# Two-layer diffusion backbone on one core: weight splits and modulation accumulation in instructions of 1024 columns in place of 512

## The chip, the core and the metric

The program runs on one core of one Trainium2 chip. The metric is the time of one execution on the device in microseconds (us), as the median of several runs. The work is fp32 throughout, and every input comes from device memory in each execution.

## The reference

Two layers work on 256 latent tokens (and in layer 0 on 256 context tokens beside them), with a model width of 1024 and a hidden width of 2816. A layer is a half-step SwiGLU FFN, a token mixer (layer 0: neighbourhood attention; layer 1: a short gated convolution), and a second half-step FFN. Each sub-layer is modulated by rows that come from a conditioning vector.

```python
m = (silu(c) @ ada_w[i] + ada_b[i]).reshape(B, N_MOD, 1, D)      # nine rows a layer
...
def half_step_ffn(x, shift, scale, gate, w_in, w_out, g, b):
    a, u = split(modulate(x, shift, scale) @ w_in, 2)             # x * (1 + scale) + shift
    y = (silu(a) * u) @ w_out
    return layer_norm(ALPHA * x + 0.5 * gate * y, g, b)
...
x = half_step_ffn(x, m[0], m[1], m[2], ffn_w_in[i, 0], ffn_w_out[i, 0], ...)
x = post_norm_update(x, mixer(modulate(x, m[3], m[4])), m[5], 1.0, ...)
x = half_step_ffn(x, m[6], m[7], m[8], ffn_w_in[i, 1], ffn_w_out[i, 1], ...)
```

In attention a latent token reads a window of the latent grid and all context keys in one softmax. The weights are read once each: 5632 columns in and 2816 rows out for each of four FFNs, 3072 and 1024 columns for each mixer, and 9216 columns of `ada_w` a layer.

## The kernel before

**Split products.** TensorE (PE) multiplies in a reduced fp32 form (`fp32r`). To keep the accuracy, each operand is stored as a high part, rounded to that form, and a low part, the rest. A product is three matmuls: high by high, high by low and low by high (`mmu`, lines 152 to 159). A weight comes in units of 256 rows by 512 columns, which lie in a tile as 128 partitions by 1024 columns (`wunit`). The program calls the raw unit `w1r`, `w2r`, `wor` and so on, its high part `w1h`, its low part `w1l`. ScalarE (ACT) makes the high part (line 178) and VectorE (DVE) the low part (line 181), each in two instructions of 512 columns, as `W_HI` and `W_LO` are 2. There are four buffers for raw units and five for each part (`WB`), with a few more in some phases.

**Activations.** Between sub-layers a normalised tile is transposed on PE into PSUM (`hT`), scaled and shifted by ACT in four instructions of 128 columns (`h`, line 340), and split by ACT (`hTh`, line 105) and DVE (`hTl`, line 106). `panels` then runs over panels of 512 columns of the FFN's first weight (256 for silu, 256 for the factor), four units each, for two token tiles; `lead_in` gives the order of the first two panels. `done` of `gated` makes `sil`, the product of both halves (DVE, line 386), which PE transposes (line 394). `out_gemm` multiplies by the second weight, `w2`, or by `wo` after a mixer.

**The first FFN** holds its activations transposed (`f0_mm`) and starts while its own modulation is computed (`start_step`). The units of its first two panels are split in that phase.

**Modulation rows.** The other rows are made in the background by `ada`: 128 rows of `ada_w` for one modulation vector (1024 columns) are loaded as `ar`, and DVE multiplies them by one element of silu(c) per partition and adds them up in `acc`, a first product (line 241) and seven updates (line 243) for each vector, each in two halves of 512 columns. Ones on PE then sum `acc` over the partitions. A step of it is released after so many matmul groups (`tick`, the background rate).

**Attention** (layer 0) runs in steps of a head and a query tile: scores S on PE (line 814), a bias and the row's maximum on DVE, the exponential on ACT (line 818) and its scaling `pr` (line 820), four transposes PT on PE (line 832), the split into `pT` (lines 105 and 106), and the values o (PE, lines 844 and 845), collected by ACT as `osum` (line 850). The key, query and value projections of later heads (`wkv`, `wq`; `kT` is the transposed key, line 769) and the first units of `wo` are filled in between these steps.

**The order of the work.** PE's instructions stand in the order of the program text, by hand. Those of the other engines are ordered by a scheduler from priorities; `tc.high_priority` moves a block of them forward by a number of places. Weight splits are moved by `w_early`, the activation's splits by `LN_EARLY`, the softmax and what follows it by `S_EARLY`, `P_EARLY` and `V_EARLY`. Each engine runs its own queue from front to back.

Of the kernel before, what the change touches and what calls it, by code (L numbers as in the profile page):

```python
# [9 lines left out]
F32 = mybir.dt.float32  # L10
F32R = mybir.dt.float32r
AF = mybir.ActivationFunctionType
ALU = mybir.AluOpType
# [3 lines left out]
P = 128  # L17
D = 1024
# [34 lines left out]
AHEAD = 3  # L53
P_EARLY = 70
V_EARLY = 70
W_HI = 2
W_LO = 2
NA = (1, 2, 1, 0, 0, 0)
NB = (2, 2, 1, 0, 0, 0)
E0 = (0,)  # L60
# [4 lines left out]
def backbone_kernel(  # L65
# [6 lines left out]
    nc = tc.nc  # L72
# [8 lines left out]
    hp = phase.__enter__()  # L81
# [2 lines left out]
    w_early = [0]  # L84
    ext = [1, 0]
    ada_late = [0]

    def nm(s):
        uid[0] += 1
        return f"{s}_{uid[0]}"  # L90
# [54 lines left out]
    def set_background(gen, rate):  # L145
        background[:] = [gen, rate, 0.0]
# [15 lines left out]
    def wunit(srcs, kn, s):  # L162

        raw = wp.tile([P, UN], F32, tag="wr", bufs=WB[0], name=nm(s + "r"))
        ext[1] += 1
        if ext[0] and ext[1] % (5 + ext[0]) in (E0 if ext[0] == 1 else E2):
            hi = hp.tile([P, UN], F32R, tag="whx", bufs=ext[0], name=nm(s + "h"))
            lo = hp.tile([P, UN], F32R, tag="wlx", bufs=ext[0], name=nm(s + "l"))
        else:
            hi = wp.tile([P, UN], F32R, tag="wh", bufs=WB[1], name=nm(s + "h"))  # L170
            lo = wp.tile([P, UN], F32R, tag="wl", bufs=WB[2], name=nm(s + "l"))
        rv, hv, lv = (t[:, :kn * 512].rearrange("p (a b) -> p a b", a=kn) for t in (raw, hi, lo))
        with tc.high_priority(offset=w_early[0]):
            for src, c in srcs:
                sync.dma_start(rv[:, :, c:c + src.shape[2]], src)
            m = kn * 512
            for a in range(0, m, m // W_HI):
                nc.scalar.activation(hi[:, a:a + m // W_HI], raw[:, a:a + m // W_HI], AF.Copy)  # L178
            for a in range(0, m, m // W_LO):
                b = a + m // W_LO  # L180
                nc.vector.tensor_tensor(out=lo[:, a:b], in0=raw[:, a:b], in1=hi[:, a:b].bitcast(F32), op=ALU.subtract)  # L181
        return hv, lv

    def wrows(w, r0, n, c0, s):
        src = w[r0:r0 + n * P, c0:c0 + 512].rearrange("(k p) n -> p k n", p=P)
        return wunit([(src, 0)], n, s)

    def wpair(w, u, c0, c1, s):
        if c1 == c0 + 256:
            return wrows(w, u * UK * P, UK, c0, s)  # L190
        src = w[u * UK * P:(u + 1) * UK * P, :].rearrange("(k p) n -> p k n", p=P)
        return wunit([(src[:, :, c0:c0 + 256], 0), (src[:, :, c1:c1 + 256], 256)], UK, s)
# [7 lines left out]
    cst = cp.tile([P, KC, 32], F32, tag="cst", name="cst")  # L200
# [10 lines left out]
    ones = cp.tile([P, 32], F32, tag="ones", name="ones")  # L211
# [4 lines left out]
                            in1=idv[:, 1, :, 0:2], op=ALU.add)  # L216
# [7 lines left out]
    def ada(vecs):  # L224


        acc = {}
        for l, m in dict.fromkeys((l, m) for l, m, _ in vecs):
            for k in range(KC):
                w = hp.tile([P, D], F32, tag="ar", bufs=3, name=nm("ar"))  # L230
                sync.dma_start(w, ada_w[l, k * P:(k + 1) * P, m * D:(m + 1) * D])
                for i, vec in enumerate(vecs):
                    if vec[:2] != (l, m):
                        continue
                    if k == 0:
                        acc[i] = [hp.tile([P, 512], F32, tag="acc", bufs=4, name=nm("acc")) for _ in range(2)]
                    sc = cst[:, k, vec[2]:vec[2] + 1]
                    for h in range(2):
                        src, a = w[:, h * 512:(h + 1) * 512], acc[i][h]
                        if k == 0:  # L240
                            nc.vector.tensor_scalar(a, src, sc, None, op0=ALU.mult)
                        else:
                            nc.vector.scalar_tensor_tensor(out=a, in0=src, scalar=sc, in1=a,  # L243
                                                           op0=ALU.mult, op1=ALU.add)
                yield 1
        n = 2 * len(vecs)
        bt = hp.tile([P, 512], F32, tag="adab", name=nm("adab"))
        for i, (l, m, v) in enumerate(vecs):
            sync.dma_start(bt[64 * i:64 * i + 64],
                           bass.AP(ada_b.tensor, ada_b.offset + (l * 9 + m) * D, [[512, 2], [0, 32], [1, 512]]))  # L250
        yield 1
        yield 1
        yield 1
        rows = hp.tile([P, 512], F32, tag="adar", name=nm("adar"))
        ps = tpb("ada")
        for i in range(len(vecs)):
            for h in range(2):
                j = 2 * i + h
                nc.tensor.matmul(ps[32 * j:32 * j + 32, :], ones, acc[i][h], start=True, stop=True)
        nc.vector.tensor_tensor(out=rows[:32 * n], in0=ps[:32 * n], in1=bt[:32 * n], op=ALU.add)  # L260
        for i, (l, m, v) in enumerate(vecs):
            sync.dma_start(scr[l][v, m * D:(m + 1) * D].rearrange("(a b) -> a b", b=512),
                           rows[64 * i:64 * i + 64:32, :])
        yield 1

    def stream(*groups):
        for g in groups:
            yield from ada(g)
# [91 lines left out]
    def panels(cols, w, hTs, order, done, s):  # L360

        units, banks = {}, {}
        for t, p, u in order:
            if (p, u) not in units:
                units[p, u] = wpair(w, u, *cols[p], s)
            if (t, p) not in banks:
                banks[t, p] = mmb(s, t)
            hi, lo = units[p, u]
            mmu(banks[t, p], [(*hsl(hTs[t], UK * u + i), hi[:, i], lo[:, i]) for i in range(UK)], u == 0, u == KU - 1)
            if u == KU - 1:  # L370
                done(p, t, banks.pop((t, p)))
            yield
            tick()
# [71 lines left out]


    w_in, w_out = ffn_w_in[0, 0], ffn_w_out[0, 0]
    ab0 = [hp.tile([P, 512], F32, tag="acc", bufs=4, name=nm("ab0")) for _ in range(2)]
    for h in range(2):
        nc.vector.memset(ab0[h], 0.0)  # L450
    xt = []
    for t in range(4):
        if t < 2:
# [103 lines left out]
    for q, (k0, n) in enumerate(steps):  # L557
        nxt = start_step(*steps[q + 1]) if q < 4 else iter(())
        for g in range(6):
# [9 lines left out]
    sync.dma_start(win_sb, win_mask)  # L569
    sync.dma_start(rope, rope_tab.rearrange("(t p) a b -> p t a b", p=P))  # L570
    w_early[0] = W_EARLY
    set_background(stream([(0, 2, 0), (0, 2, 1)], [(0, 3, 0), (0, 3, 1)], [(0, 4, 0), (0, 4, 1)],
                          [(0, 5, 0), (0, 6, 0)], [(0, 7, 0), (0, 8, 0)], [(1, 0, 0)]), 0.45)
    ada_late[0] = 0
# [287 lines left out]
    hp = phase.__enter__()  # L862
# [35 lines left out]
    for i in range(len(steps) + LAG + V_LAG):  # L898
# [13 lines left out]
        n = int(credit)  # L912
# [10 lines left out]
        j = i - LAG - V_LAG  # L923
# [8 lines left out]
    hp = phase.__enter__()  # L932
# [20 lines left out]
    w = sc_w_in[0]  # L953
# [104 lines left out]
```

## Time and profile before

| before | |
|---|---|
| three runs, median | 1293.48 us (1292.49 to 1294.41) |
| the profiled execution's own time | 1290.21 us |
| its span on the core | 1288.4 us |
| mean granted clock of TensorE | 0.996 |
| loaded from device memory | 267.93 MB |
| DMA packets' time on the main queue, share of 16 engines' span | 66.9% |

The profile is of one execution, and its durations are in microseconds unless they say ns. Busy time is counted per engine: PE (matmul), PEld (PE's weight load, which overlaps the matmuls), DVE, ACT, POOL (GpSimd). A group of instructions names the line, the engine, the operation, the tiles (written <- read, without their numbers), the shape and the count; behind the bar stand its busy time, the mean of one in ns, and the idle time of the engine in front of them with what ended most of it. In a list of waits a row is engine, tile and line <- what released it, then the total, the number of waits and the longest. In a timeline a row has the start, the length, the engine, the line, the operation and tiles, and a count of instructions that follow each other; in brackets is the wait before it. Instructions of DVE and ACT overlap in their records, so a start-to-start distance is shorter than a length.

### The profile page before, as it was taken

How to read it: one execution, taken by the hardware profiler on the slowest of the kernel's cores; microseconds unless marked ns; L12 is line 12 of the kernel's file. 1: busy time of each engine (PE TensorE's matmuls, PEld its weight loads, DVE VectorE, ACT ScalarE, POOL GpSimd, SP SyncE). 2: the span in 40 equal slices, each digit the busy share in tenths (PEclk: the TensorE clock that was granted, in tenths of full speed). 3: DMA queues.
4: the chain of work that ended last, by engine and by line, in shares of the span. 5: the costliest groups of instructions: out<-in, count | busy, mean ns of one | idle time of the engine just before them, and what ended most of it. 6: DMA issues, size and time to landing. Idle time of an engine off the chain costs nothing.

```text
span 1288.4 us, 17192 instructions
## 1 busy us (share of the span) xinstructions
PE 1256.5 (98%) x5890; PEld 1005.4 (78%) x5890; DVE 954.7 (74%) x1683; ACT 591.0 (46%) x1148; POOL 40.4 (3%) x69
## 2 busy tenths in 40 slices
PE   7999999999999999988999999999999999999997
PEld 4787778788778877766787787887788877788886
DVE  3599877595658767788997888867878688855545
ACT  2433132412326456677554535645435645655431
POOL 0000000000001111120000000000000000000000
PEclk9999999999999999989999999999999999999999
DMA  9978668484622744464998988677887764676641
GB/s 285 284 238 260 187 187 289 153 299 150 216 66 85 217 90 90 92 149 130 314 333 267 325 315 298 205 220 222 290 298 244 211 218 147 214 213 187 226 158 50
DMA packets 204018, 271.26 MB, mean 211 GB/s; under 512 B 30028, under 2 KB 149300, under 8 KB 203930
## 3 DMA queue, kind: packets, MB, share of 16 engines
q1 hardware_dynamic: 203930, 270.16, 66.9%
q8 instruction: 46, 0.75, 0.2%
q14 instruction: 42, 0.34, 0.1%
HBM read 267.93 MB, written 2.17 MB: 210 GB/s over the span
## 4 chain that ended last, share of the span: by engine, by line
PE 81%; DVE 7%; DMA 6%; ACT 3%; issue 1%; SPq 1%; POOL 0%; DVEq 0%; ACTq 0%
PE w L156 15%; PE w L157 14%; PE w L159 14%; PE f L537 6%; PE f L539 6%; PE f L538 6%; DMA w1r<-in_ffn_w_in_dram 4%; DVE w1l L181 2%; PE wkv L156 2%; PE wkv L159 2%; PE wkv L157 2%; PE wc L156 2%; PE wc L157 2%; PE wc L159 2%; DMA ar<-in_ada_w_dram 1%
## 5 line engine op out<-in xcount | busy, mean ns | idle before, releaser
L178 ACT ACTIVATE w1h<-w1r 128x512 fp32r<-128x512 f32 x352 | 203.1, 626 | 185.7 <-PE w L159 71.4
L181 DVE TENSOR_TENSOR w1l<-w1r,w1h 128x512 fp32r<-128x512 f32 x352 | 227.6, 685 | 66.7 <-ACT w1h L178 63.5
L156 PE MATMUL w<-w1h,hTh 128*128 128x512 f32 x528 | 210.8, 399 | 3.3 <-ACT hTh L105 3.3
L243 DVE SCALAR_TENSOR_TENSOR acc<-ar,cst,acc 128x512 f32<-128x512 f32 x266 | 187.5, 746 | 33.6 <-DMA ar<-in_ada_w_dram 33.3
L157 PE MATMUL w<-w1l,hTh 128*128 128x512 f32 x528 | 207.0, 392 | 0.0
L156 PE MATMUL w<-w2h,gh 128*128 128x512 f32 (+1 forms) x446 | 175.4, 394 | 0.0
L157 PE MATMUL w<-w2l,gh 128*128 128x512 f32 (+1 forms) x446 | 173.4, 389 | 0.0
L178 ACT ACTIVATE w2h<-w2r 128x512 fp32r<-128x512 f32 x176 | 101.5, 624 | 140.9 <-PE w L159 122.2
L159 PE MATMUL w<-w1h,hTl 128*128 128x512 f32 x528 | 163.4, 391 | 0.7 <-DVE hTl L106 0.7
L181 DVE TENSOR_TENSOR w2l<-w2r,w2h 128x512 fp32r<-128x512 f32 x176 | 114.0, 686 | 42.1 <-ACT w2h L178 41.4
L537 PE MATMUL f<-h0h,w1h 128*128 128x512 f32 x352 | 139.3, 396 | 0.0
L539 PE MATMUL f<-h0l,w1h 128*128 128x512 f32 x352 | 137.8, 392 | 0.0
L538 PE MATMUL f<-h0h,w1l 128*128 128x512 f32 x352 | 137.8, 391 | 0.0
L159 PE MATMUL w<-w2h,gl 128*128 128x512 f32 (+1 forms) x446 | 136.3, 387 | 0.0
L156 PEld LDWEIGHTS w<-w1h,hTh 128*128 128x128 f32 x528 | 99.2, 188 | 27.2 <-ACT hTh L105 4.6
L159 PEld LDWEIGHTS w<-w1h,hTl 128*128 128x128 f32 x528 | 98.9, 188 | 23.9 <-DVE hTl L106 1.5
L157 PEld LDWEIGHTS w<-w1l,hTh 128*128 128x128 f32 x528 | 99.2, 188 | 20.3 <-DVE w1l L181 0.3
L156 PEld LDWEIGHTS w<-w2h,gh 128*128 128x128 f32 x446 | 83.7, 188 | 21.8 <-issue 1.7
L159 PEld LDWEIGHTS w<-w2h,gl 128*128 128x128 f32 x446 | 83.3, 188 | 18.8
L157 PEld LDWEIGHTS w<-w2l,gh 128*128 128x128 f32 x446 | 83.7, 188 | 17.4
L537 PEld LDWEIGHTS f<-h0h,w1h 128*128 128x128 f32 x352 | 66.2, 188 | 17.9 <-issue 4.1
L539 PEld LDWEIGHTS f<-h0l,w1h 128*128 128x128 f32 x352 | 66.2, 188 | 14.4
(176 smaller groups left out, 1703.1 us busy)
## 6 DMA issues: line engine op xcount, KB each, us to landing
w1r<-in_ffn_w_in_dram SPq DMA_DIRECT2D x352, 256.0 KB
ar<-in_ada_w_dram SPq DMA_DIRECT2D x128, 512.0 KB
w2r<-in_ffn_w_out_dram SPq DMA_DIRECT2D x88, 512.0 KB
ar<-in_ada_w_dram SPq DMA_DIRECT2D x32, 256.0 KB
wkvr<-in_na_w_qkv_dram SPq DMA_DIRECT2D x32, 256.0 KB
wcr<-in_sc_w_in_dram SPq DMA_DIRECT2D x32, 256.0 KB
wqr<-in_na_w_qkv_dram SPq DMA_DIRECT2D x8, 512.0 KB
bias<-in_na_rpb_dram SPq DMA_DIRECT2D x64, 64.0 KB
```

The source lines that it names most:

```text
L156: nc.tensor.matmul(ps, lh, rh, start=first and i == 0, stop=False)
L157: nc.tensor.matmul(ps, lh, rl, start=False, stop=False)
L159: nc.tensor.matmul(ps, ll, rh, start=False, stop=last and i == n - 1)
L178: nc.scalar.activation(hi[:, a:a + m // W_HI], raw[:, a:a + m // W_HI], AF.Copy)
L181: nc.vector.tensor_tensor(out=lo[:, a:b], in0=raw[:, a:b], in1=hi[:, a:b].bitcast(F32), op=ALU.subtract)
L243: nc.vector.scalar_tensor_tensor(out=a, in0=src, scalar=sc, in1=a, op0=ALU.mult, op1=ALU.add)
L537: nc.tensor.matmul(ps, lh, hT0[k][0], start=(k == 0), stop=False)
L538: nc.tensor.matmul(ps, ll, hT0[k][0], start=False, stop=False)
L539: nc.tensor.matmul(ps, lh, hT0[k][1], start=False, stop=(k == KC - 1))
```

## The change

A unit of a weight is split by one ACT instruction and one DVE instruction of 1024 columns where `whole[0]` is set, and by two of each of 512 columns otherwise. `whole[0]` is off until the first FFN's early panels (its first two) have their units, and it is off for panel 0 of every later `panels` (three FFNs and the convolution's first weight). `acc` becomes one tile of 1024 columns for a vector, with two buffers in place of four halves; a product or an update is one instruction. PE reads the two halves of `acc` as before. The start's `ab0` takes one of these tiles and one memset.

```diff
-W_HI = 2
-W_LO = 2
...
+    whole = [False]
...
             m = kn * 512
-            for a in range(0, m, m // W_HI):
-                nc.scalar.activation(hi[:, a:a + m // W_HI], raw[:, a:a + m // W_HI], AF.Copy)
-            for a in range(0, m, m // W_LO):
-                b = a + m // W_LO
+            n = m if whole[0] else 512
+            for a in range(0, m, n):
+                nc.scalar.activation(hi[:, a:a + n], raw[:, a:a + n], AF.Copy)
+            for a in range(0, m, n):
+                b = a + n
                 nc.vector.tensor_tensor(out=lo[:, a:b], in0=raw[:, a:b], in1=hi[:, a:b].bitcast(F32), op=ALU.subtract)
...
                     if k == 0:
-                        acc[i] = [hp.tile([P, 512], F32, tag="acc", bufs=4, name=nm("acc")) for _ in range(2)]
-                    sc = cst[:, k, vec[2]:vec[2] + 1]
-                    for h in range(2):
-                        src, a = w[:, h * 512:(h + 1) * 512], acc[i][h]
-                        if k == 0:
-                            nc.vector.tensor_scalar(a, src, sc, None, op0=ALU.mult)
-                        else:
-                            nc.vector.scalar_tensor_tensor(out=a, in0=src, scalar=sc, in1=a,
-                                                           op0=ALU.mult, op1=ALU.add)
+                        acc[i] = hp.tile([P, D], F32, tag="acc", bufs=2, name=nm("acc"))
+                    sc, a = cst[:, k, vec[2]:vec[2] + 1], acc[i]
+                    if k == 0:
+                        nc.vector.tensor_scalar(a, w, sc, None, op0=ALU.mult)
+                    else:
+                        nc.vector.scalar_tensor_tensor(out=a, in0=w, scalar=sc, in1=a, op0=ALU.mult, op1=ALU.add)
...
-                nc.tensor.matmul(ps[32 * j:32 * j + 32, :], ones, acc[i][h], start=True, stop=True)
+                nc.tensor.matmul(ps[32 * j:32 * j + 32, :], ones, acc[i][:, h * 512:(h + 1) * 512], start=True, stop=True)
...
             if (p, u) not in units:
+                whole[0] = p > 0
                 units[p, u] = wpair(w, u, *cols[p], s)
+                whole[0] = True
...
     w_early[0] = W_EARLY
+    whole[0] = True
```

The order of PE's instructions does not change. On ACT and DVE some do. In the rows below an instruction is line, operation, tile written <- tiles read, with the tiles' numbers and the size; line numbers of the changed kernel are one to four lower.

The **first place** is ACT's queue in attention, from about 545 to 559 us of the profiled execution. `woh` is the high part of a unit of `wo`, `kr` and `v` belong to the key and value projection of later heads, `S`, `pr` and `mx` to the softmax. Before:

```order
L178 ACTIVATE woh_5253<-wor_5252 128x512 x2
L756 ACTIVATE kr_4971<-wkv_4885 128x256
L105 ACTIVATE v_4973<-wkv_4885 128x4x64
L105 ACTIVATE pT_4892<-PT_4976 128x4x128
L105 ACTIVATE pT_4926<-PT_4983 128x4x128
L818 ACTIVATE pr_4946,mx_4944<-S_4935,mx_4944 128x512
L818 ACTIVATE pr_4953,mx_4951<-S_4936,mx_4951 128x512
L820 ACTIVATE pr_4946<-pr_4946,mx_4944 128x512
L850 ACTIVATE osum_4999<-o_4990 64x256
L820 ACTIVATE pr_4953<-pr_4953,mx_4951 128x512
L178 ACTIVATE woh_5374<-wor_5373 128x512
```

And in the changed kernel:

```order
L178 ACTIVATE woh_4982<-wor_4981 128x1024
L756 ACTIVATE kr_4706<-wkv_4620 128x256
L104 ACTIVATE v_4708<-wkv_4620 128x4x64
L104 ACTIVATE pT_4627<-PT_4711 128x4x128
L104 ACTIVATE pT_4661<-PT_4718 128x4x128
L178 ACTIVATE woh_5101<-wor_5100 128x1024
L850 ACTIVATE osum_4734<-o_4725 64x256
L818 ACTIVATE pr_4681,mx_4679<-S_4670,mx_4679 128x512
L818 ACTIVATE pr_4688,mx_4686<-S_4671,mx_4686 128x512
L820 ACTIVATE pr_4681<-pr_4681,mx_4679 128x512
L820 ACTIVATE pr_4688<-pr_4688,mx_4686 128x512
L104 ACTIVATE pT_4767<-PT_4769 128x4x128
```

The unit `woh`, which followed the softmax, now stands ahead of it as a whole, and so does `osum`, which stood between the two scalings.

The **second place** is ACT's queue at the entry of layer 1's first FFN, at about 800 us, where the first `h` is made. Before:

```order
L178 ACTIVATE w1h_7452<-w1r_7451 128x512 x2
L178 ACTIVATE w1h_7498<-w1r_7497 128x512 x2
L178 ACTIVATE w1h_7514<-w1r_7513 128x512
L340 ACTIVATE h_7353<-hT_7348,gcol_6975 128x128 x4
L340 ACTIVATE h_7367<-hT_7362,gcol_6975 128x128
L105 ACTIVATE hTh_7354<-h_7353 128x512
```

And in the changed kernel:

```order
L178 ACTIVATE w1h_7018<-w1r_7017 128x512 x2
L178 ACTIVATE w1h_7064<-w1r_7063 128x1024
L178 ACTIVATE w1h_7078<-w1r_7077 128x1024
L337 ACTIVATE h_6921<-hT_6916,gcol_6575 128x128 x4
L337 ACTIVATE h_6935<-hT_6930,gcol_6575 128x128
L104 ACTIVATE hTh_6922<-h_6921 128x512
```

Of the unit that stands directly in front of `h`, one half stood there before, and the whole now.

The **third place** is DVE's queue in the first panels of layer 0's second FFN, at about 617 us, in front of the first `hTl` of the second token tile. Before:

```order
L181 TENSOR_TENSOR w1l_5702<-w1r_5700,w1h_5701 128x512 x2
L181 TENSOR_TENSOR w1l_5718<-w1r_5716,w1h_5717 128x512 x2
L386 TENSOR_TENSOR sil_5669<-sil_5669,w_1047_5611 128x256
L241 TENSOR_SCALAR acc_5650<-ar_5648,cst 128x512
L241 TENSOR_SCALAR acc_5651<-ar_5648,cst 128x512
L243 SCALAR_TENSOR_TENSOR acc_5650<-ar_5731,cst,acc_5650 128x512
L106 TENSOR_TENSOR hTl_5679<-h_5677,hTh_5678 128x512
```

And in the changed kernel:

```order
L181 TENSOR_TENSOR w1l_5419<-w1r_5417,w1h_5418 128x1024
L181 TENSOR_TENSOR w1l_5433<-w1r_5431,w1h_5432 128x1024
L385 TENSOR_TENSOR sil_5386<-sil_5386,w_1034_5330 128x256
L239 TENSOR_SCALAR acc_5369<-ar_5367,cst 128x1024
L241 SCALAR_TENSOR_TENSOR acc_5369<-ar_5444,cst,acc_5369 128x1024
L105 TENSOR_TENSOR hTl_5396<-h_5394,hTh_5395 128x512
```

Ahead of `hTl` stand the same operations, with the update of `acc` as a whole where only its first half stood there before.

More of the change, by code (lines that the diff above doesn't have):

```diff
@@ L447, in backbone_kernel @@
     w_in, w_out = ffn_w_in[0, 0], ffn_w_out[0, 0]
-    ab0 = [hp.tile([P, 512], F32, tag="acc", bufs=4, name=nm("ab0")) for _ in range(2)]
-    for h in range(2):
-        nc.vector.memset(ab0[h], 0.0)
+    ab0 = hp.tile([P, D], F32, tag="acc", bufs=2, name="ab0")
+    nc.vector.memset(ab0, 0.0)
+    ab0 = [ab0[:, h * 512:(h + 1) * 512] for h in range(2)]
     xt = []
```

## The prediction

> **What bounds the kernel now.** I read the page's busy times first, then the groups of instructions with shapes kept apart, then what TensorE (PE) waited for, then the clock by stretch, and only then single instructions around PE's waits.
>
> ```profile
> PE 1256.5 (98%) x5890; PEld 1005.4 (78%) x5890; DVE 954.7 (74%) x1683; ACT 591.0 (46%) x1148; POOL 40.4 (3%) x69
> PE 81%; DVE 7%; DMA 6%; ACT 3%; issue 1%; SPq 1%; POOL 0%; DVEq 0%; ACTq 0%
> L181 DVE TENSOR_TENSOR w1l<-w1r,w1h 128x512 fp32r<-128x512 f32 x352 | 227.6, 685 | 66.7 <-ACT w1h L178 63.5 <-DMA w1r<-in_ffn_w_in_dram 0.4
> L157 PE MATMUL w<-w1l,hTh 128*128 128x512 f32 x528 | 207.0, 392 | 0.0
> L157 PE MATMUL w<-w2l,gh 128*128 128x512 f32 x434 | 170.3, 392 | 0.0
> ```
>
> PE is busy for 98% of the span. The matmuls that read a split weight's low part (w1l, w2l) never had PE idle in front of them: 0.0 us in both groups. So the 227.6 us that VectorE (DVE) spends on w1l are hidden behind PE, and making them cheaper gains nothing by itself.
>
> ```profile
> PE ada L490 <- DMA ar<-in_ada_w_dram: 3.8, 4, 1.9
> PE xT L500 <- DMA x<-in_x_dram: 3.7, 2, 2.3
> PE w L156 <- ACT hTh L105: 3.3, 3, 2.0
> PE ctp L209 <- DMA crow<-in_c_ctx_dram: 2.6, 1, 2.6
> PE kT L769 <- DVE pT L106: 2.0, 2, 1.6
> PE o L845 <- DVE pT L106: 1.6, 3, 0.6
> ...
> 540.00:560.00 20.00, 16.72 (x100) 12.77 (x99) 17.07 (x37) 17.87 (x41) 4.44 (x5) 0.96 0.51 88
> 560.00:580.00 20.00, 19.41 (x102) 14.97 (x100) 14.54 (x33) 12.98 (x29) 4.39 (x6) 0.87 0.64 164
> ```
>
> The first rows are what PE waited for (total, times, longest). Three of the four longest are loads at the start or a transposed activation; then come kT and o, inside attention, which wait for DVE's split of the transposed probabilities. The last two rows are stretches (length, busy us and instructions of PE, weight load, DVE, ScalarE (ACT), GpSimd, then granted clock, DMA share, GB/s). The clock is below 1 there. The missing 0.04 and 0.13 of 20 us are 3.4 us of PE time, which at half rate is 6.8 us of throttled clock. What this kernel can still gain lies in such short waits and in this dip, some 15 us in all; nowhere else does an instruction of DVE or ACT set the time.
>
> **The change part by part. Prices first.**
>
> ```profile
> 603.45 2.48 DVE L181 TENSOR_TENSOR w1l<-w1r,w1h 128x512 fp32r<-128x512 f32 x4
> 605.85 0.68 DVE L304 SCALAR_TENSOR_TENSOR res<-wo,gate 128x512 f32<-128x512 f32 x1
> 614.84 0.41 DVE L386 TENSOR_TENSOR sil<-sil,w 128x256 f32<-128x256 f32 x1
> 615.18 0.88 DVE L241 TENSOR_SCALAR acc<-ar,cst 128x512 f32<-128x512 f32 x2
> 615.97 0.75 DVE L243 SCALAR_TENSOR_TENSOR acc<-ar,cst,acc 128x512 f32<-128x512 f32 x1
> 616.63 0.69 DVE L106 TENSOR_TENSOR hTl<-h,hTh 128x512 fp32r<-128x512 f32 x1
> ...
> 616.11 0.68 ACT L178 ACTIVATE w1h<-w1r 128x512 fp32r<-128x512 f32 x1
> 616.63 0.68 ACT L105 ACTIVATE hTh<-h 128x512 fp32r<-128x512 f32 x1
> 557.63 0.41 ACT L105 ACTIVATE oT<-osum 128x256 fp32r<-128x256 f32 x1
> 557.93 0.60 ACT L105 ACTIVATE kTh<-kT 128x512 fp32r<-128x512 f32 x1
> ```
>
> Queued instructions overlap, so a price is start to start. On DVE four splits take 605.85 - 603.45 = 2.40 us, 0.60 each; the 256-column product takes 615.18 - 614.84 = 0.34. That is 1.02 ns a column and 0.08 fixed, so 1024 columns are estimated at 1.12 us against 1.20 for two halves. An acc update takes 616.63 - 615.97 = 0.66; for the whole the bounds are 1.18 (only columns added) and 1.32 (nothing saved), and I take 1.24. The two first products take 0.79 together, the whole between that and 0.71. On ACT a half takes 616.63 - 616.11 = 0.52 and 256 columns 557.93 - 557.63 = 0.30: 0.96 for a whole against 1.04.
>
> The change merges 304 pairs of splits on ACT and on DVE, and 152 pairs of acc on DVE (counted in the programs' order). Saved are 304 x 0.08 = 24 us of ACT and 456 x 0.08 = 36 us of DVE, off the path, since PE's 0.0 us above hide them. The DMAs are as many, of the same sizes. The early panels and each panel 0 keep 512 columns. The merged memset of ab0 stands in a start where PE waits for loads: nothing.
>
> What is on the path is the other side: whatever stands behind a whole has to wait 0.44 us longer on ACT and up to 0.52 (a split) or 0.6 (an acc) on DVE, and a low part can't begin before the whole high part is written.
>
> ```profile
> 799.51 0.63 ACT L178 ACTIVATE w1h<-w1r 128x512 fp32r<-128x512 f32 x1 [2.12 <-DMA w1r<-in_ffn_w_in_dram]
> 800.05 1.84 ACT L340 ACTIVATE h<-hT,gcol 128x128 f32<-128x128 f32 x5
> 802.46 0.50 PE L156 MATMUL w<-w1h,hTh 128*128 128x512 f32 x1 [2.02 <-ACT hTh L105]
> 1085.21 3.75 ACT L178 ACTIVATE w1h<-w1r 128x512 fp32r<-128x512 f32 x7 [4.79 <-DMA w1r<-in_ffn_w_in_dram]
> 1091.31 0.50 PE L156 MATMUL w<-w1h,hTh 128*128 128x512 f32 x1 [0.64 <-ACT hTh L105]
> 617.37 0.74 PE L159 MATMUL w<-w1h,hTl 128*128 128x512 f32 x2 [0.32 <-DVE hTl L106]
> 589.64 0.39 PE L845 MATMUL o<-pT,v 128*128 128x256 f32 x1 [0.42 <-DVE pT L106]
> 706.64 0.44 PE L394 MATMUL gT<-ident,sil 128*128 128x128 f32 x2 [0.56 <-DVE sil L386]
> ```
>
> *At 800 us* ACT waits 2.12 us for a weight's load, splits its first half, and only then does the h that PE needs. Now the whole stands there (the second place shown in the change): +0.44, behind a wait of PE that is already open, so all of it counts. If the load comes earlier, as some ada loads are moved past it, this could be -1.5 (about one load's turn); I keep +0.44, the row that is there. *At 1085* seven halves (3.64) become three wholes and two halves (3.92): +0.28. *At 617* hTl has in front of it two wholes of w1l (-0.16), the first product (nothing) and a whole acc (+0.58): +0.4. *At 589* a whole woh stands ahead of two pT where halves alternated with them: +0.4. *At 706* the second sil stands behind a whole acc (+0.58), three wholes ahead of it gave back 0.24; a first pair at 694 has its split start 0.2 later: +0.5 together. If each of these were hidden again, they would be 0; if each were followed by the DVE step behind it, about twice as much.
>
> *Attention, 550 to 559 us:*
>
> ```profile
> 551.28 0.71 ACT L818 ACTIVATE pr<-S,mx 128x512 f32<-128x512 f32 x1
> 552.74 0.28 PE L845 MATMUL o<-pT,v 128*128 128x256 f32 x1
> 553.85 0.66 PE L832 MATMUL PT<-ident,pr 128*128 128x128 f32 x4
> 555.17 0.28 PE L845 MATMUL o<-pT,v 128*128 128x256 f32 x1
> 558.52 1.11 PE L769 MATMUL kT<-ident,kr 128*128 128x128 f32 x4 [1.56 <-DVE pT L106]
> 559.56 0.79 PE L810 MATMUL S<-kTh,qTh 64*128 64x512 f32 x2
> ```
>
> In the new order ACT's osum, which reads the o that ends at 553.0, stands ahead of the softmax pr, which began at 551.28 (first place shown). So the softmax begins some 1.5 to 2 us later, and PE's transposes PT at 553.85 wait about 1.3. But the two woh halves that stood between it and the kT at 558.52 are gone from there, so the 1.56 us there shrink; followed by hand through ACT and DVE, kT comes at about 559.0: +0.5. The bounds are -1 (kT gains all that was moved away) and +1.5.
>
> The sum of these: 0.44 + 0.28 + 0.4 + 0.4 + 0.5 + 0.5 = +2.5 us.
>
> *The clock dip.* From 555.17 to 559.56 PE does only transposes and waits, 4.4 us, and the half clock follows. In the new order the o ends about 1.3 later and the scores begin 0.5 later: 3.6 us, and broken by the moved transposes. I take it that this is too short a lull to trigger the dip: -3.4 us, between 0 and 3.4. [...]
>
> Sum against the profiled execution: 1290.21 + 2.5 - 3.4 = 1289.3 (its span is 1288.4, 1.8 us lie around it). The median of the runs shown is 1293.48, 3.3 us above that execution; the same -0.9 on it gives **1292.6 us**. About 0.2%, or 2.6 us, is what a measurement of this kernel can tell from no change.
>
> [...]
>
> **The rivals.** *Relief reaches PE's waits.* DVE is 74% busy over all, and in attention PE's waits end on it. If DVE's 36 us less let kT's 2.0 us of waiting vanish together with the dip, and the late starts above are hidden, it is -2.0 - 3.4 = -5.4: 1288.1. For it: DVE never rests long from 540 to 560 (17.07 of 20 us busy). Against it: ACT, not DVE, was late there by its order, and its new order is no shorter. Chance 0.28.
>
> *The dip stays.* [...] Then +2.5: 1296.0, at the edge of what can be told. Chance 0.20. That the merging does nothing at all to PE (the waits as long, the dip there) is the mild end of it, 1293.5.
>
> *A second dip.* [...] Chance 0.10.
>
> **How the numbers follow.** The forecast has 0.42, the rivals 0.28, 0.20 and 0.10. The forecast's terms have bounds from about -2.5 to +2.5 around it, so 0.05 of its 0.42 fall below -2.6 us and 0.03 above. Faster: 0.28 + 0.05 = 0.33. Same: 0.34 and 0.08 of the case in which the dip stays, 0.42. Slower: 0.03 + 0.12 + 0.10 = 0.25. The range goes from 1287.0, a little below relief's 1288.1, to 1298.0, beyond the 1296.0 of a dip that stays and short of the second dip; the forecast's own is 1290 to 1295.5. What lies outside is about 2 in 10.
>
> **What would show it.** Prices: L181 and L178 of 1024 columns about 1.12 and 0.96 us apart; DVE busy some 36 us less, ACT 24, PE still at 98%. Late starts: the first h behind an unbroken split at the entry of each sub-layer, and PE's wait for hTh at 802 longer by 0.4. The dip: a granted clock of 1.00 in all stretches from 540 to 580; if it is below, that step is wrong. Attention: PE's wait in front of PT near 554, and a shorter one in front of kT. Wrong would be the whole reading if PE waited for w1l or w2l anywhere, or if its matmuls came closer together than now in the stretches without waits.

## The result and the profile after

| | before | after |
|---|---|---|
| median of four runs beside each other | 1293.32 us (1292.49 to 1294.41) | 1308.79 us (1304.03 to 1310.39) |
| ratio, 95% interval | | 1.0103 (1.0073 to 1.0134) |
| profiled execution, its span | 1290.21, 1288.4 us | 1304.03, 1302.2 us |

The changed kernel is slower: by 1.0% in the measured ratio, by 15.5 us (1.2%) in the medians, and by 13.8 us in the two profiled executions. The page's busy times and the groups of the two matmuls that read low parts, of the kernel after:

```profile
PE 1262.6 (97%) x5890; PEld 1008.5 (77%) x5890; DVE 915.9 (70%) x1226; ACT 563.4 (43%) x844; POOL 41.6 (3%) x69
...
L156 PE MATMUL w<-w1l,hTh 128*128 128x512 f32 x528 | 207.0, 392 | 0.2 <-DVE w1l L181 0.2
L156 PE MATMUL w<-w2l,gh 128*128 128x512 f32 (+1 forms) x446 | 173.5, 390 | 0.0
```

DVE did its work in 38.8 us less, ACT in 27.6 us less, and the time didn't gain by it. The clearest rows are those of the long stretch from 40 to 400 us (length, busy us and count of PE, weight load, DVE, ACT and GpSimd, then granted clock, DMA share, GB/s), first of the kernel before:

```profile
40.00:400.00 360.00, 360.00 (x1623) 289.16 (x1621) 268.17 (x439) 108.41 (x192) 1.49 (x4) 1.00 0.65 207
```

and after:

```profile
40.00:400.00 360.00, 360.00 (x1619) 289.16 (x1618) 252.59 (x287) 101.38 (x127) 1.49 (x4) 1.00 0.65 207
```

PE is busy for all 360 us in both, while DVE has 15.6 us less to do. So the loss is elsewhere. PE's longest waits after (total, times, longest; those for the loads of the start left out):

```profile
PE w L155 <- ACT hTh L104: 4.8, 3, 3.1
PE hT L331 <- DVE x L323: 4.3, 5, 1.2
...
PE o L845 <- DVE pT L105: 2.4, 3, 1.0
PE kT L769 <- DVE pT L105: 1.8, 1, 1.8
PE S L810 <- DVE kTl L105: 1.7, 2, 1.0
PE o L844 <- ACT pT L104: 1.0, 2, 0.8
...
PE S L810 <- ACT pr L818: 0.9, 1, 0.9
PE qT L787 <- DVE qr L711: 0.8, 1, 0.8
```

The row that counts most is the second: the transposes hT wait for the normalised x from DVE, 4.3 us where it was 1.0. The row of before:

```profile
PE hT L334 <- DVE x L326: 1.0, 2, 0.7
```

PE runs the same 5890 matmuls in the same order in both kernels. So the start of a matmul after, less its start before, says how much was lost up to there, and the difference of two such numbers says what a stretch lost. For instance the hT that began at 602.53 begins at 610.27 after: 7.7 us lost by then. By stretches (times of before):

| stretch, us | 0 to 45 | to 545 | to 602 (end of attention) | to 790 | to 822 (entry of layer 1) | to 990 | to 1112 (entries of the mixer and the last FFN) | rest |
|---|---|---|---|---|---|---|---|---|
| lost, us | 1.5 | 1.2 | 5.0 | -0.6 | 3.2 | 0.2 | 3.5 | 0.0 |

**The entries.** DVE's timeline after at about 815 us (start, length, line, operation, then the wait before it), and the transpose that waits for it:

```profile
812.85 0.69 DVE L305 SCALAR_TENSOR_TENSOR x<-x,res 128x512 f32<-128x512 f32 x1
813.52 1.23 DVE L181 TENSOR_TENSOR w1l<-w1r,w1h 128x1024 fp32r<-128x1024 f32 x1
814.67 0.68 DVE L105 TENSOR_TENSOR hTl<-h,hTh 128x512 fp32r<-128x512 f32 x1
815.27 0.69 DVE L307 BATCH_NORM_STATS2 st<-x 128x6 f32<-128x512 f32 x1
815.87 1.21 DVE L181 TENSOR_TENSOR w1l<-w1r,w1h 128x1024 fp32r<-128x1024 f32 x1
817.00 0.20 DVE L314 BATCH_NORM_AGGREGATE mv<-st 128x2 f32<-128x12 f32 x1
818.13 1.00 DVE L323 TENSOR_SCALAR x<-x,mv,rs 128x512 f32<-128x512 f32 x2 [0.93 <-POOL rs L317]
...
818.73 1.11 PE L331 MATMUL hT<-ident,x 128*128 128x128 f32 x8 [1.21 <-DVE x L323]
```

The same steps before:

```profile
803.77 0.69 DVE L308 SCALAR_TENSOR_TENSOR x<-x,res 128x512 f32<-128x512 f32 x1
804.53 0.69 DVE L106 TENSOR_TENSOR hTl<-h,hTh 128x512 fp32r<-128x512 f32 x1
805.14 0.69 DVE L310 BATCH_NORM_STATS2 st<-x 128x6 f32<-128x512 f32 x1
805.74 0.68 DVE L181 TENSOR_TENSOR w1l<-w1r,w1h 128x512 fp32r<-128x512 f32 x1
806.33 0.20 DVE L317 BATCH_NORM_AGGREGATE mv<-st 128x2 f32<-128x12 f32 x1
806.45 0.64 DVE L181 TENSOR_TENSOR w1l<-w1r,w1h 128x512 fp32r<-128x512 f32 x1
807.80 1.00 DVE L326 TENSOR_SCALAR x<-x,mv,rs 128x512 f32<-128x512 f32 x2 [0.71 <-POOL rs L320]
```

A layer norm goes over DVE in steps: residual, statistics, their sum, the normalised x. Before, the first half of a weight's split filled the gap between the statistics and their sum, and the second half ran for nothing while GpSimd made the root. A whole can't be cut in that way: it stands ahead of the sum with all of its length, and another one ahead of hTl. From the residual to x it is 5.28 us after and 4.03 before, and PE waits 1.2 us where the view of before shows no wait. At 1012 us it is the same again (1.2 us), and at 1110 us PE waits 0.5 us.

**The end of attention.** ACT's row of the whole woh, its two pT behind it, DVE's pT, and what PE waited for, after:

```profile
591.20 1.04 ACT L178 ACTIVATE woh<-wor 128x1024 fp32r<-128x1024 f32 x1
592.14 1.07 ACT L104 ACTIVATE pT<-PT 128x512 fp32r<-128x512 f32 x2
...
592.27 1.23 DVE L181 TENSOR_TENSOR wol<-wor,woh 128x1024 fp32r<-128x1024 f32 x1 [1.48 <-ACT woh L178]
593.41 1.28 DVE L105 TENSOR_TENSOR pT<-PT,pT 128x512 fp32r<-128x512 f32 x2
...
592.78 0.39 PE L844 MATMUL o<-pT,v 128*128 128x256 f32 x1 [0.77 <-ACT pT L104]
594.15 0.39 PE L845 MATMUL o<-pT,v 128*128 128x256 f32 x1 [0.99 <-DVE pT L105]
```

Before, halves of woh and wol alternated with the pT, and PE waited 0.56 us (in front of the last transposes PT) and 0.42 us there. The clock then fell. Three stretches of the kernel after (the third number from the end is the granted clock):

```profile
591.29:594.70 3.41, 1.65 (x10) 1.15 (x10) 2.42 (x3) 1.92 (x4) 0.00 (x0) 1.00 0.04 6
594.70:598.11 3.41, 2.49 (x12) 2.20 (x11) 0.42 (x1) 0.38 (x1) 0.00 (x0) 0.50 0.47 147
...
585.00:605.00 20.00, 16.80 (x72) 12.94 (x71) 10.88 (x24) 7.90 (x17) 0.00 (x0) 0.74 0.17 53
```

In 20 us with a mean clock of 0.74, 5.2 us of PE's clock are missing, where the kernel before had 1.00 in the same stretch. Over the span the mean granted clock of the four runs is 0.990 to 0.992; the profiled execution before has 0.996.

### The profile page after: what moved, and what is told of

Its sections match the earlier page's. It is cut to its first block, busy times and chain, and to the rows that moved or that the text cites. A ratio compares the mean times of both kernels' runs of the same rounds, so it can differ in the third digit from the quotient of the medians.

```text
span 1302.2 us, 16417 instructions
## 1 busy us (share of the span) xinstructions
PE 1262.6 (97%) x5890; PEld 1008.5 (77%) x5890; DVE 915.9 (70%) x1226; ACT 563.4 (43%) x844; POOL 41.6 (3%) x69
## 4 chain that ended last, share of the span: by engine, by line
PE 76%; DMA 10%; DVE 8%; issue 2%; ACT 2%; SPq 1%; POOL 0%; DVEq 0%; ACTq 0%
PE w L155 13%; PE w L156 13%; PE w L158 13%; PE f L536 6%; PE f L538 6%; PE f L537 6%; DMA w1r<-in_ffn_w_in_dram 4%; DMA ar<-in_ada_w_dram 4%; DVE w1l L181 2%; PE wkv L155 2%; PE wkv L156 2%; PE wc L155 2%; PE wkv L158 2%; PE wc L156 2%; PE wc L158 2%
## 5 line engine op out<-in xcount | busy, mean ns | idle before, releaser
L181 DVE TENSOR_TENSOR w1l<-w1r,w1h 128x1024 fp32r<-128x1024 f32 (+1 forms) x196 | 215.7, 1110 | 89.6 <-ACT w1h L178 88.5
L178 ACT ACTIVATE w1h<-w1r 128x1024 fp32r<-128x1024 f32 (+1 forms) x196 | 188.3, 973 | 193.7 <-PE w L158 93.4
L241 DVE SCALAR_TENSOR_TENSOR acc<-ar,cst,acc 128x1024 f32<-128x1024 f32 x133 | 168.7, 1281 | 40.2 <-DMA ar<-in_ada_w_dram 39.3
L178 ACT ACTIVATE w2h<-w2r 128x1024 fp32r<-128x1024 f32 x88 | 93.4, 1062 | 144.7 <-PE w L158 130.3
L181 DVE TENSOR_TENSOR w2l<-w2r,w2h 128x1024 fp32r<-128x1024 f32 x88 | 106.7, 1221 | 50.2 <-ACT w2h L178 49.0
```

The costliest lines, as they stand in the source:

```text
L178: nc.scalar.activation(hi[:, a:a + n], raw[:, a:a + n], AF.Copy)
L241: nc.vector.scalar_tensor_tensor(out=a, in0=w, scalar=sc, in1=a, op0=ALU.mult, op1=ALU.add)
```

## The experiments

Each run is compared with runs of the kernel before on the same chip (medians 1293.2, 1293.7, 1292.5 and 1292.2 us in the four groups). The theory: wholes cost where they stand between the steps of a short chain. Its rivals: the updates of acc, the longest instructions of DVE, are what delays; or the half clock falls by chance.

**Weights only, acc only.** The first keeps the whole splits and puts `acc` back into two tiles and two instructions; the second keeps `acc` whole and never sets `whole[0]`.

> Theory Q (the time comes from weight splits of 1024 columns that stand between the steps of a short chain on ACT or DVE): the splits are all still whole, so nearly all of the loss stays, about 1307 us (1305 to 1310), with PE's waits for the normalised x of about 0.7 to 1.2 us at the three entries and the wait at the end of attention. Rival A (the update of acc, at 1.28 us the longest instruction of DVE, is what delays): the loss goes, about 1295. Rival C (the loss is half-clock stretches that fall by chance): anywhere from 1300 to 1309, by the half clock in its trace.

1305.28 us, ratio 1.0100 (1.0074 to 1.0127). With acc in halves PE still waits for the normalised x at the three entries: 1.2 us at 817, 1.2 at 1012 and 0.5 at 1111 us. These waits belong to the weights' splits.

> Theory Q: 1293 to 1295, within 1.5 us of the kernel before, no wait of PE for the normalised x above 0.4 us. Rival A: 1304 or more. Rival C: 1290 to 1300, by the half clock in its trace alone.

1295.88 us, ratio 1.0019 (1.0006 to 1.0033), 0.9 us above theory Q's range, with one wait of 3.4 us for x in its trace, not 0.4 at most. The splits make most of the loss, but acc isn't free. The place in the trace of the kernel with acc alone:

```profile
791.07 0.69 DVE L307 BATCH_NORM_STATS2 st<-x 128x6 f32<-128x512 f32 x1
795.27 0.69 DVE L181 TENSOR_TENSOR w1l<-w1r,w1h 128x512 fp32r<-128x512 f32 x1 [3.51 <-ACT w1h L178]
795.88 0.20 DVE L314 BATCH_NORM_AGGREGATE mv<-st 128x2 f32<-128x12 f32 x1
```

It is the same gap between the statistics and their sum, filled with a split, here of 512 columns, whose high part comes 3.51 us late. The loads and their order on the issuing queue are not those of before. So length is one price of what stands in that gap, and lateness another; that the order of the loads made it late was not tried by itself.

**Attention's weights in halves; its wo alone in halves.**

```diff
     phase.__exit__(None, None, None)
+    whole[0] = False
     ext[0] = 0
```

> Only the splits of attention's weights (wkv, wq, wo) go back to halves. Theory Q: the 6.4 us that PE lost between 415 and 605 us come back, half of them as the half clock near 595 us that no longer has a lull to start in: about 1302 to 1303, the entries after 790 us lose as much as in the changed kernel. Rival A: no change, 1308. Rival C: the half clock near 595 us stays, or falls elsewhere, 1305 to 1309.

1300.68 us, ratio 1.0052 (1.0033 to 1.0071): 8.1 us of the loss are gone.

```diff
     def wrows(w, r0, n, c0, s):
+        if s == "wo" and ext[0] == 0:
+            whole[0] = False
```

> The changed kernel with only the splits of attention's wo in halves; wkv and wq stay whole. Theory Q: the whole woh and wol stand between the transposed probabilities at 550 to 600 us, so the half clock there goes back to that of the kernel before (mean granted clock 0.995 or more in place of 0.991), and about 6 of attention's 8.1 us come back: 1302 to 1304; the waits for qT and kTl at 420 to 447 us stay, 1.7 us. Rival (wkv and wq decide): 1306 to 1309, clock 0.991.

1301.56 us, ratio 1.0070 (1.0056 to 1.0085), mean granted clock of its six runs 0.995 to 0.997. The stretch 585 to 605 us of this kernel, with the clock at 1.00 in place of 0.74:

```profile
585.00:605.00 20.00, 16.95 (x91) 13.47 (x90) 15.24 (x33) 11.71 (x25) 1.07 (x2) 1.00 0.26 79
```

So the fall goes with wo's wholes: with them PE is busy for 1.65 of the 3.41 us in front of it, and with halves a stretch of 3.41 us with 2.02 there keeps the clock. The rival that the half clock falls there by chance has all the traces against it: a half clock near 594 us stands in each of the four kernels whose low parts of attention's wo are whole (the changed one, weights only, panel 1 in halves, low parts and acc whole) and in none of the other thirteen traces; the mean granted clock of the four profiled executions is 0.990 to 0.993, of the thirteen 0.993 to 0.999. Against the runs of before on its own chip this kernel loses 9.1 us and attention in halves 7.5, where the change lost 15.5: wo's wholes make most of attention's share.

**Panel 1 in halves.**

```diff
-                whole[0] = p > 0
+                whole[0] = p > 1
```

> Only the splits of panel 1 go back to halves, beside those of panel 0. Theory Q: the 6.8 us that PE lost at the entries (796 to 820, 1000, 1090 to 1100 us) come back, since two splits of panel 1 stand in DVE's chain from the residual to the normalised x and one on ACT ahead of h: about 1302, with PE's waits for x of at most 0.3 us each; attention loses as before. Rival A: no change, 1308. Rival C: no change beyond the half clock in its trace.

1302.14 us, ratio 1.0068 (1.0045 to 1.0090). The entries at 1000 and 1090 to 1110 us lose nothing against before (0.0 in place of 3.5 us). At 803 us a wait of 1.9 us for x stays, behind a split of 512 columns whose high part came 1.82 us late, as with acc alone.

**One engine at a time.** In the line of the high part (first) or of the low part (second) the step is 512 in place of n.

> The changed kernel with the high parts in halves on ACT; the low parts and acc stay whole on DVE. Theory Q with DVE's queue as the place (normalised x, hTl, kTl, pT wait there): half to two thirds of the loss stays, 1300 to 1304, and PE's waits for the normalised x at about 818, 1012 and 1110 us are as in the changed kernel; the wait for hTh near 810 shrinks by 0.4. Rival ACT (the whole high part is what delays): 1293 to 1297.

1306.04 us, ratio 1.0082 (1.0058 to 1.0106), 2 us above the expected range: its trace, of the slowest of its six runs, loses 4.4 us at the end of attention and 3.6 and 2.9 us at the entries, like the changed kernel, and 4.2 us more between 602 and 790 us.

> The changed kernel with the low parts in halves on DVE; the high parts stay whole on ACT, and acc whole on DVE. Theory Q with DVE's queue as the place: the waits for the normalised x at 818, 1012 and 1110 us go back to at most 0.4 us, and what is left is ACT's part and acc's: 1297 to 1301. Rival ACT: as slow as the changed kernel, 1305 to 1309.

1299.45 us, ratio 1.0041 (1.0024 to 1.0058). The low parts on DVE decide at the end of attention (-0.6 us with halves there), and halves of them take back 1.9 of the 3.5 us at the entries from 1000 us on. The waits for x at 818 and 1110 us are gone; at 1009 us one of 0.8 us stays, twice what was expected.

> Only the high parts are whole (ACT), the low parts and acc are in halves. Theory that DVE's instructions are what delays: ACT's share alone is the 2 to 3 us that the halves on ACT gave back: 1294 to 1298. Rival ACT: 1300 or more, with the wait for hTh near 803 us at 2.5 us or longer as the only large one.

1301.38 us, ratio 1.0064 (1.0048 to 1.0079), 3 us over the expected range. The time is the rival's, but not its sign: the wait for hTh at 807 us is 2.0 us. Its trace has a loss of 5.0 us between 822 and 990 us, where the changed kernel loses 0.2. By the medians the high parts alone cost 8.9 us and the low parts with acc 12.3, more than the 15.5 of all together; the intervals, some 2 to 4 us wide on each side, do not settle whether the parts add up.

**Wholes in the rest only**, where no chain was thought to be: panels from 2 on, w2 and layer 1's wo, with acc in halves.

> Attention's splits, those of panels 0 and 1, and acc go back to halves; only the splits of the panels from 2 on and of the second FFN weights and layer 1's wo stay whole. Theory Q (wholes cost only where they stand between the steps of a short chain): the shares of the parts add up, 8.1 us (attention) and 6.7 us (panel 1) of the 15.6 us, so that about 0.8 is left with acc: 1292 to 1295, the same as before. Rival L (low parts of wholes come too late for the loads that run close, w2l at 960 to 980 us): a loss of 2 to 4 us stays, 1295 to 1297, with waits of PE for w2l. Rival C (half clock by chance): 1290 to 1300.

1297.32 us, ratio 1.0022 (1.0004 to 1.0040): the theory in its first form falls. The rival that w2l comes too late is left, but its sign isn't in this trace, where PE waits 0.9 us for w2l: the profiled execution took 1291.31 us, the least of the twelve runs.

> The kernel with wholes in the rest only (1297.3), with the high parts in halves everywhere, so that only low parts of the later panels, w2 and layer 1's wo are whole. If the 3.6 us that were left there come from the whole high parts: 1293 to 1295. If from the whole low parts: 1296 to 1298, with waits of PE for sil or w2l.

1297.21 us, ratio 1.0028 (1.0012 to 1.0043).

> The kernel with wholes in the rest only (1297.3), with the low parts in halves everywhere, so that only high parts of the later panels, w2 and layer 1's wo are whole. If the 3.6 us that were left there come from the whole low parts: 1293 to 1295. If from the whole high parts: 1296 to 1298.

1298.74 us, ratio 1.0043 (1.0027 to 1.0058). Either half of that change alone costs as much as both. DVE and PE of the latter, at about 982 us:

```profile
976.02 2.49 DVE L181 TENSOR_TENSOR w2l<-w2r,w2h 128x512 fp32r<-128x512 f32 x4
981.42 0.75 DVE L243 SCALAR_TENSOR_TENSOR acc<-ar,cst,acc 128x512 f32<-128x512 f32 x1 [2.90 <-DMA ar<-in_ada_w_dram]
...
983.95 0.69 DVE L181 TENSOR_TENSOR w2l<-w2r,w2h 128x512 fp32r<-128x512 f32 x1
...
984.69 0.50 PE L156 MATMUL w<-w2l,gh 128*128 128x512 f32 x1 [1.99 <-DVE w2l L181]
```

DVE stood 2.90 us before an update of acc whose load was late, with the w2l that PE needed behind it. Two runs test that: w2 in halves too, and the updates of acc further back (`ADA_LATE` 40 in place of 20, in the kernel with the low parts alone).

> The kernel with wholes in the rest only (1297.3), with w2 in halves as well, so that only the later panels (p from 2 on) and layer 1's wo are whole. Theory R (between 945 and 982 us an update of acc that waits for its load stands at the head of DVE's queue, and a whole w2l behind it comes too late): PE's waits for w2l there go below 1 us in total, and the time to 1292 to 1294.5. Rival (the order of the loads is moved by the other wholes): 1296 to 1298, with waits for w2l as before that.

1292.07 us, ratio 0.9989 (0.9976 to 1.0002): as fast as before, with 168 units split whole. The row of PE's waits for w2l in the kernel with the low parts alone, and then that of this kernel:

```profile
PE w L156 <- DVE w2l L181: 5.0, 5, 2.6
```

```profile
PE w L156 <- DVE w2l L181: 0.2, 1, 0.2
```

> The kernel whose later low parts alone are whole (1297.2; PE waited 5.0 us for w2l), with the updates of acc 40 places later in the scheduler's priorities in place of 20. Theory R: fewer of them stand ahead of the w2l that PE needs, the waits for w2l fall to 2 us or less, 1293 to 1295.5. Rival (the loads come too late in any order): waits as before, 1296 to 1299.

1297.83 us, ratio 1.0040 (1.0023 to 1.0057). PE's waits for w2l between 940 and 990 us fell from 4.2 to 2.6 us, and the time did not. So w2's wholes are the cause of what was left in the kernel with wholes in the rest, while whether they act by their length, by their order beside acc or by the loads that they hold up is open. In the changed kernel's own trace, where w2 is whole too, that stretch (822 to 990 us) lost only 0.2 us.

**The first FFN alone.**

> Wholes only in the first FFN (up to about 415 us), halves and acc in halves behind it. In the changed kernel PE lost and won nothing between 45 and 415 us. Theory that DVE's and ACT's saved time is worth nothing where they are hidden: within 1.5 us of the kernel before, 1292 to 1294.5, and no step of PE above 0.4 us behind 45 us other than by the half clock. Rival (any change of the order costs): 1295 or more.

1294.38 us, ratio 1.0009 (0.9994 to 1.0025): no difference that can be measured. Behind the first FFN its instructions on PE, ACT and DVE stand in the order of before, and yet PE waited 0.9 us for w2l at 975 us: some loss in that stretch comes without any change of length or order there.

**The other way: quarters.** In the kernel before, the splits of attention and of panels 0 and 1 in instructions of 256 columns.

> The other way: the kernel before, with the splits of attention's weights and of panels 0 and 1 in quarters of 256 columns. Theory Q: what stands between the steps of a chain gets 0.27 us shorter at each place, against some 100 instructions with 0.08 us more each that PE does not see: 1289 to 1292, faster by 1 to 4 us. Rival F (the fixed part of an instruction counts in attention, where DVE is busy for 85%): 1294 to 1298. Rival C: anything within 3 us, by the half clock in its trace.

1298.77 us, ratio 1.0029 (1.0015 to 1.0044). Attention gained nothing, and from 602 to 790 us 5.1 us were lost, with PE waiting for DVE's sil and w1l (3.7 more up to 822 us, with a half clock of 6.83 us at 808):

```profile
PE gT L396 <- DVE sil L388: 3.2, 4, 1.4
...
PE w L156 <- DVE w1l L181: 1.8, 2, 1.6
```

So shorter isn't better either. The likely reason, which was not tried by itself, is that more instructions carry more fixed cost (0.08 us each, estimated from the start-to-start rows in the prediction) where DVE has no room; from 620 to 640 us it is busy for 19.13 of 20 us in the kernel before:

```profile
620.00:640.00 20.00, 20.00 (x93) 16.44 (x92) 19.13 (x33) 8.87 (x18) 0.00 (x0) 1.00 0.96 324
```

Where each kernel's profiled execution lost, in us against that of before, found as above:

| kernel | 0 to 45 | to 545 | to 602 | to 790 | to 822 | to 990 | to 1112 |
|---|---|---|---|---|---|---|---|
| changed | 1.5 | 1.2 | 5.0 | -0.6 | 3.2 | 0.2 | 3.5 |
| weights only | 0.8 | 1.7 | 5.2 | 0.6 | 0.4 | 2.0 | 3.3 |
| acc only | -0.4 | 0.0 | -1.4 | -0.3 | 4.2 | 2.6 | 0.2 |
| attention in halves | 1.7 | 0.9 | -3.0 | -1.0 | 4.2 | 2.7 | 3.6 |
| wo in halves | 3.0 | 1.5 | -2.9 | 0.7 | 3.4 | 2.5 | 3.8 |
| panel 1 in halves | -0.2 | 1.3 | 5.1 | -1.2 | 2.6 | 1.5 | 0.0 |
| low parts and acc whole | 2.3 | -0.1 | 4.4 | 4.2 | 3.6 | 2.0 | 2.9 |
| high parts and acc whole | 3.2 | 0.7 | -0.6 | 0.6 | 2.7 | 2.0 | 1.6 |
| high parts alone | 3.2 | 0.5 | -1.1 | 1.6 | 1.1 | 5.0 | 2.0 |
| rest, w2 in halves | 2.3 | 0.6 | -2.5 | 0.4 | -0.6 | 0.6 | 0.0 |
| rest | -0.7 | 1.2 | -1.6 | 1.4 | -0.2 | 1.6 | 0.1 |
| rest, low parts whole | -0.1 | 0.0 | -1.6 | 0.7 | 2.0 | 7.5 | 0.1 |
| rest, high parts whole | 2.2 | 0.1 | -1.9 | 2.8 | 0.2 | 6.4 | 0.1 |
| rest, low parts, acc later | 3.7 | 0.0 | -1.6 | 1.8 | 3.1 | 3.6 | 0.2 |
| first FFN alone | 1.0 | 0.1 | -1.9 | 0.1 | -0.4 | 1.4 | 0.4 |
| quarters | 0.1 | -0.4 | 0.0 | 5.1 | 3.7 | 1.5 | -0.4 |

Three columns are clear.

- To 602 us the loss goes with whole low parts of wo: 4.4 to 5.2 us with them, and at most 0.0 without. The negative numbers come from the kernel before: its profiled execution has a half clock of 6.83 us at 558 us, and all the others but quarters have one of 3.41 us or none there.
- To 1112 us it goes with the splits of panel 1: 2.9 to 3.8 us with whole low parts, 1.6 and 2.0 with whole high parts alone, and at most 0.4 with neither.
- To 822 us it goes with whole acc: the seven kernels with it lose 2.6 to 4.2 us, and each has a wait for x near 800 us, of 0.5 to 3.4 us. With acc in halves the loss is 2.0 us at most, except with acc later (3.1) and in quarters (3.7). Of the changed kernel's 3.2 us in this stretch, the kernel with the same splits and acc in halves loses only 0.4, though it has the wait of 1.2 us at 817 us.

The first column is hardly the kernels' doing, for their start differs by one memset at most. The columns to 790 and 990 us show no rule: to 990 us acc alone, with w2 in halves, loses 2.6 us, and the changed kernel 0.2. Late loads stand there (2.90 us above). Each row is one execution.

## Why the prediction was wrong

- **The prices were right.** Start to start, three whole low parts take 445.14 - 441.74 = 3.40 us after, 1.13 each (1.12 was said), two updates of acc 953.70 - 951.17 = 2.53, 1.27 each (1.24). On ACT a whole high part takes 809.14 - 808.18 = 0.96 (0.96). DVE saved 38.8 us (36), ACT 27.6 us (24).

```profile
441.74 3.49 DVE L181 TENSOR_TENSOR wkvl<-wkvr,wkvh 128x1024 fp32r<-128x1024 f32 x3
445.14 0.42 DVE L105 TENSOR_TENSOR v<-wkv,v 128x256 fp32r<-128x256 f32 x1
...
951.17 2.60 DVE L241 SCALAR_TENSOR_TENSOR acc<-ar,cst,acc 128x1024 f32<-128x1024 f32 x2 [2.06 <-DMA ar<-in_ada_w_dram]
953.70 0.18 DVE L290 COPY gcol<-mcT 128x32 f32<-128x32 f32 x1
...
808.18 1.06 ACT L178 ACTIVATE w1h<-w1r 128x1024 fp32r<-128x1024 f32 x1 [1.68 <-DMA w1r<-in_ffn_w_in_dram]
809.14 1.84 ACT L337 ACTIVATE h<-hT,gcol 128x128 f32<-128x128 f32 x5
```

- **"Off the path" was right for the gain.** It is worth nothing: 40 to 400 us, and wholes in the first FFN alone. One sign that was named as speaking against the whole reading did come, a wait of PE for w1l, but once and of 0.2 us; it is too small to carry the loss.
- **The step that failed first is the list of late starts** ("What is on the path is the other side"). It went through the places where PE waited in the trace of before, and gave +2.5 us. Left out were the places where PE did not wait, but with a slack smaller than the 0.5 us by which a whole is longer. Those are the layer norms, with wholes in two of their gaps: PE waits 1.2 us at 818 and at 1012 us, and 0.5 us at 1110 us. These waits stand with acc in halves too, and with panel 1 in halves all three are gone. The entry of the mixer at 1000 us, which lost 1.7 us, wasn't on the list at all.
- **Single places of the list:** at 802 us the term itself came: `h` begins 0.96 us behind the start of a whole where it was 0.54 behind that of a half, +0.42 where +0.44 was said. But PE's wait for hTh grew by 1.04, from 2.02 to 3.06 us, as the load came later too, and in the kernel with the weights alone, with the same splits, it is 1.12: the load decides there. ACT kept to its order in both kernels: `h` stood behind a split that had waited 2.12 us for its load before, and 1.68 after. At 1091 us the wait for hTh grew from 0.64 to 0.93 us, as the +0.28 said, and one of 0.45 us for hTl came behind it, the DVE step for which about twice as much was allowed. At 617 us the wait for hTl is 0.29, as before, not +0.4. At 706 us the stretch gained where +0.5 was said. At 589 us waits of 0.77 and 0.99 us stand where 0.56 and 0.42 stood, +0.8 where +0.4 was said. From 550 to 559 us the softmax did come late, with a wait of 0.9 us in front of S where 1.3 in front of PT was said, but the wait in front of kT did not shrink: 1.8 us where 1.6 stood.
- **The clock dip went the other way.** It was to vanish, -3.4 us: the step that failed is that a lull of 3.6 us with transposes in it is too short to trigger it, an estimate of the author's that no run shows. After, the half clock came at 557 us for 3.41 us (6.83 before), and at 594.7 us for 10.24 us: 6.8 us of PE's clock, where the kernel before lost 3.4. In the 3.41 us in front of these two PE was busy for 1.95 and 1.65 us. The rival of a second dip had the sign, with a chance of 0.10; it came at 594 us, where the list had +0.4 us. Attention's end lost 5.0 us, where +0.5 and +0.4 less 3.4 were said. That the whole low parts of wo cause it is shown by the kernel with wo in halves and by the four traces that have it.
- **The order's part was seen and not priced.** That loads of ada_w move past others was named at 800 us, as a possible gain of 1.5 us. With acc alone whole the time is 2.7 us longer (1295.88 against 1293.16), and the stretch around 800 us loses with whole acc in each of seven traces. That the loads' order does it is argued from the late split, not shown.

What stays open: how w2's wholes delay w2l, since moving the updates of acc took back the waits in part and no time, and how whole acc delays the split at 800 us.

## What to carry to other kernels

- Fixed cost saved on engines that are hidden behind PE bought nothing here: DVE did its work in 38.8 us less, ACT in 27.6 us less, and the median is 15.5 us longer. What a longer instruction costs is read where it fills a gap between two steps of a chain: look for chains with slack under the added length, not only for waits that are there already.
- A scheduler that fills a gap can take a half of 0.60 us and hide the other half in the next gap; of a whole of 1.13 us it can't. So size such filler by the shortest gap of the chains it shares an engine with, and use larger ones only where no chain passes (168 units here, for no gain).
- Don't count on the parts of such a change to add up: the high parts alone lost 5.0 us in a stretch where the changed kernel lost 0.2, each in one execution. Put parts back alone and together, compare the start of the same matmul in both traces, and trust a stretch only where several kernels agree.

## What the runs showed of the hardware

**The half clock came without an idle stretch.** From 591.29 to 594.70 us PE was busy for 1.65 of 3.41 us, with transposes and matmuls of 256 columns, and the next 10.24 us ran at half rate (a granted clock of 0.50), though in the first 3.41 us of these it was busy for 2.49. In the kernel before, too, the window in front of the dip has PE busy for 1.58 us, so the trace at hand could have told it:

```profile
554.96:558.37 3.41, 1.58 (x13) 1.11 (x11) 2.92 (x5) 3.36 (x8) 0.73 (x1) 1.00 0.83 165
```

From 589.38 to 592.79 us of the kernel with wo in halves it was busy for 2.02 us, and the clock stayed:

```profile
589.38:592.79 3.41, 2.02 (x14) 1.46 (x12) 3.04 (x5) 2.37 (x5) 0.00 (x0) 1.00 0.51 152
```

Up to 1280 us the traces of before and of the changed kernel have four half clocks: of 3.41 us (from 38.33 and from 557.16 us after), 6.83 us (from 558.37 before) and 10.24 us (from 594.70 after). In the 3.41 us in front of them PE was busy for 1.84, 1.95, 1.58 and 1.65 us in that order, 46 to 57%. Three other stretches of 3.41 us with as little were followed by full clock: 1.66 us from 800.71 us before, 1.63 from 560.57 and 1.60 from 809.74 us after. So PE's busy time alone doesn't tell where the clock falls; what does is open.

**Whether it falls varies from execution to execution.** Of 17 traces, 8 have a half clock of 3.41 us that begins between 38 and 42 us, in a start that differs by one memset at most. The changed kernel's trace is one of them, and up to 45 us it lost 1.5 of its 13.8 us. Attention in halves lost 1.7 us there without a half clock; PE waited 5.2 us for the start's `ar` in it, where it waited 3.8 before. The kernel with wholes in the first FFN alone has the instructions of before in their order at 558 us, and a half clock of 3.41 us there in place of 6.83. The kernel with wholes in the rest took 1291.31 to 1301.56 us in twelve runs; its three fastest have a mean granted clock of 0.998, its three slowest of 0.994 or 0.995.
